# An attention kernel with a shorter way for the softmax shifts, a row norm in three parts, and its DFT spread over a block

## The chip, the cores and the metric

The kernel runs on one core of a Trainium2 chip. The metric is device time in microseconds (us), the median of three runs. PE is the TensorE engine, DVE is VectorE, ACT is ScalarE, POOL is GpSimd and SP is SyncE, whose queue issues most of the DMAs.

## What is computed

One layer (`DEPTH = 1`) over 4096 tokens of width 1024, with 16 meta tokens put ahead of them. Cut to what matters:

```python
u    = rmsnorm(h, norm_g)
proj = u @ w_in
f_in, f_gate, q, k, v, a_gate = split(proj)
f_out = fourier_branch(f_in, w_fmix, b_fmix) * silu(f_gate)
q, k  = rope(rmsnorm(q)), rope(rmsnorm(k))
a_out = softmax(q @ k.T / 8) @ v
h = h + concat(f_out, a_out * silu(a_gate)) @ w_out
return rmsnorm(h, final_g)[:, 16:]
```

There are 8 query heads and 2 key heads of width 64. The Fourier branch is a 2-D DFT over positions and channels, then a linear map per group.

## The kernel before

Every product of float32 numbers is made as three matmuls of 16-bit halves, a high part and the rest.

**Phase A** takes the tokens in tiles of 128, norms and projects them, and writes q, k, v and the gates to memory. **Phase B** does the rest. Its DFT is a list `flist` of 18 units of some 50 matmuls each ("pd" tiles), which `f_step(n, mid)` issues n at a time; each piece of its coefficients (`ct`) is a load of 1088 KB, and `mix` ends a unit with a product on POOL (`mo`, L834). Units are fed in as filler beside other work.

**Attention** goes in 8 blocks of 512 queries. A block has 4 pairs of heads, so there are 32 pairs, numbered from 0 here. A pair is 66 steps: two heads times 33 key tiles, the 33rd being the 16 meta keys. A step of `step` is `qk`, two matmuls on PE (L977 with the high halves `qA`, L978 with `qB`), an exp on ACT (L981), a subtraction `rr` (L983, 128x512) on DVE or POOL, and `pvm`, nine small matmuls on PE (L998 to L1005). `pvm` runs four steps (`LAG`) after its `qk`, so the products of key tile 5 stand in step 9. The last `pvm` of a head is followed by the copy `tt` on ACT and the chain `ob` of four products on POOL (L1013 to L1016). `on_dve` puts the `rr` of two steps after each place of the table `AT` on DVE, the others on POOL.

**The shifts.** Exp needs a maximum per query. While a pair runs, `max_units` finds those of the next pair: `grp` is two matmuls of 64 rows (L922) and a DVE reduce (L923), two groups at each step of `AT`; `meta` does the meta keys (L930, L932), `red` reduces to `mm` and scales to `nm` (L937, L938), and `fin` brings `nm` into rows 64 and up of `qB`: eight matmuls (L945) and two ACT copies (L948). Row 64 of `qB` meets a row of 256 in K, so L978 of a pair's first step adds the shift and needs the row to be there.

**The output projection** of a block runs in the four pairs of the next block, 128 tokens in each. At step `TR` `out_tr` transposes (L1041, into a bank of the same ring of two as the groups use) and splits (`mh` on ACT, `ml` on DVE, L1045); `out_units` puts one matmul (L1058) into each of 24 steps from `O0` and from `O1`; the sum with x is `hh` (L1063, DVE). At step 2 of the following pair `out_end` norms the tile: square on ACT (L1073), the root in ten small instructions on DVE (L1074 to L1092), then the scaled product `yo` on DVE (L1077) and its DMA.

**Block 0** has no output projection. Its 264 steps take in the rest of the DFT (`block0`, five matmuls a step from step 6 on), and after that the eight pieces of `w_out` are loaded (`wo_load`) and split on ACT and DVE (`wo_prep`, L909, L910).

**Between** phase A and block 0 lies a prelude: 50 DFT matmuls, the loads `qP` (query rows for the maxima), `wst`, `sgn` and `bias` for `fix_prep` (small DVE work on the DFT's first rows), the rest of K, then the 33 groups of pair 0 with DFT matmuls between them.

The order of work on an engine is the order of the code. The lines that set it here:

```python
AT = [0, 4, 8, 12, 15, 19, 22, 26, 29, 33, 36, 40, 43, 47, 50, 53, 56]
TR, O0, O1 = 8, 13, 41
last = {58: red, 61: fin}
on_dve = {j + 2 for j in AT}
```

Of the kernel before, what the change touches and what calls it, by code (L numbers as in the profile page):

```python
# [126 lines left out]
def phase_a(tc, a, pool, mm3, id16, id32, sc):  # L127
# [15 lines left out]
    with ExitStack() as st:  # L143
# [392 lines left out]
        early = sorted(order[:done])  # L536
        runs = [(t, t + 1) for t in early if t == NT]
        for t in early:
            if t < NT:
                if runs and runs[-1][1] == t and runs[-1][0] < NT:  # L540
                    runs[-1] = (runs[-1][0], t + 1)
                else:
                    runs.append((t, t + 1))
        at(done * 4 + 2 - 3 * 4, ld["k_load"], runs)
        ld["rest"] = sorted(order[done:])
# [118 lines left out]
def phase_b(tc, a, pool, mm3, id32, id16, sc):  # L664
# [10 lines left out]
    with ExitStack() as st:  # L675
# [14 lines left out]
        nm = [bp.tile([P, 2, 4, 32], F16, name=f"nm{i}") for i in range(2)]  # L690
# [41 lines left out]
        mo = w2.tile([P, 2, 512], F32, tag="ob", name="mo")  # L732
# [179 lines left out]

        def max_units(i):
            b, p = pairs[i]
            kv, q, n = p // 2, qP[b % 2], nm[i % 2]
            mx = sm.tile([P, 4, 2, 9], F32, tag="mx", name="mx")
# [8 lines left out]
            def meta():  # L925
                t = pm.tile([P, 2, 512], F32, tag="m", name="m")
                for e in range(2):
                    rs = slice(64 * e, 64 * e + 64)
                    for s in range(4):
                        T.matmul(t[:, e, s * 16:s * 16 + 16], q[rs, s, p], K[kv][rs, NT, 0, :NMETA],  # L930
                                 start=s == 0, stop=True, skip_group_check=s > 0)
                V.tensor_reduce(mx[:, :, :, 8], t[:, :, :64].rearrange("p e (s k)->p s e k", s=4),  # L932
                                axis=AX.X, op=ALU.max)

            def red():
                m = sm.tile([P, 4, 2], F32, tag="mm", name="mm")
# [15 lines left out]
            return [(lambda s=s, c=c: grp(s, c)) for s, c in order], meta, red, fin  # L952
# [171 lines left out]
        def block0(g, mid):  # L1124
# [5 lines left out]
            if g >= 6:  # L1130
                f_step(5, 1 if mid else 0)
# [252 lines left out]
```

## Time and profile before

| | before |
|---|---|
| median of three runs | 3383.28 us |
| the profiled execution: its own time, its span | 3382.96 us, 3381.2 us |
| phase A | 0 to 732 us |
| prelude | 732 to 824.5 us |
| pairs 0 to 3 (block 0) | 91.7, 97.8, 92.2 and 74.0 us |
| pairs 4 to 30 | 75.3 us, then 76.9 to 77.1 us each |
| pair 31 and the tail | 65.7 us and 58 us |
| busy over the span | PE 97%, DVE 70%, POOL 66%, ACT 51% |

The lengths of the pairs are distances between their first rows of L977. A row of the timeline gives the start, the duration, the engine, line, operation and tile, and in brackets the idle time of the engine ahead of it and what ended that. Matmuls overlap, so what one costs is the distance from its start to the next start.

### The profile page before, as it was taken

What the parts mean: (1) busy time and instruction counts of PE and PEld (TensorE: products, weight loads), DVE (VectorE), ACT (ScalarE), POOL (GpSimd) and SP (SyncE); (2) the same over time, 40 slices, a digit from 0 to 9 for tenths busy, and PEclk for the clock granted to TensorE, in tenths of its full rate; (3) what the DMA queues carried; (4) which work ended last, traced back from release to release, by engine and by line L of the source; (5) the groups of instructions that cost most, each with busy time, mean ns of one, the idle gap of its engine ahead of it and who ended that gap; (6) DMA issues with size and microseconds to landing.
All of it is one profiled execution on the core that took longest, in us unless ns stands there. A gap on an engine that the chain in (4) does not pass through costs nothing.

```text
span 3381.2 us, 79026 instructions
## 1 busy us (share of the span) xinstructions
PE 3278.4 (97%) x33332; PEld 1909.9 (56%) x33332; DVE 2368.1 (70%) x3249; ACT 1736.6 (51%) x3018; POOL 2226.8 (66%) x2131
## 2 busy tenths in 40 slices
PE   7999999988999999999999999999999999999998
PEld 3655555546676555555555555555555555555554
DVE  6666565537667877777777777777777776777764
ACT  5443443322555655555555555555555555555553
POOL 3655555323667877777777777777777777777762
PEclk9999999989999999999999999999999999999999
DMA  6444443437431110010001000200100010010001
GB/s 211 153 156 138 143 145 126 130 114 211 134 121 50 51 51 27 20 45 20 20 20 45 20 20 25 59 20 20 45 20 20 20 45 20 20 39 20 20 20 57
DMA packets 142298, 223.61 MB, mean 66 GB/s; under 512 B 30358, under 2 KB 85478, under 8 KB 137590
## 3 DMA queue, kind: packets, MB, share of 16 engines
q1 hardware_dynamic: 128118, 193.38, 18.3%
q10 hardware_dynamic: 13824, 25.17, 2.0%
q8 instruction: 261, 4.28, 0.5%
q14 instruction: 95, 0.78, 0.1%
HBM read 157.38 MB, written 61.14 MB: 65 GB/s over the span
## 4 chain that ended last, share of the span: by engine, by line
PE 67%; DVE 6%; issue 2%; ACT 1%; POOL 0%; ACTq 0%; POOLq 0%; DVEq 0%
PE s L977 12%; PE s L978 12%; PE o L998 11%; PE po L1058 9%; PE m L922 7%; PE o L1005 7%; PE pd L769 2%; PE o L1003 2%; PE o L1001 2%; DVE mx L923 1%; DVE yo L1077 1%; PE m L1217 1%; PE m L1041 1%; DVE r1t L1091 1%; DVE rf L1092 1%
## 5 line engine op out<-in xcount | busy, mean ns | idle before, releaser
L983 POOL TENSOR_TENSOR rr<-pe 128x512 f16<-128x512 f32 (+1 forms) x1541 | 1637.0, 1077 | 627.2 <-ACT pe L981 620.6
L981 ACT ACTIVATE pe<-s 128x512 f32<-128x512 f32 (+1 forms) x2112 | 1260.3, 597 | 1037.5 <-PE s L978 1011.1
L923 DVE TENSOR_REDUCE mx<-m 128x2 f32<-128x1024 f32 x1024 | 1206.1, 1217 | 260.8 <-PE m L922 256.9
L1005 PE MATMUL o<-VV,rr 128*128 128x65 f16 x8448 | 974.7, 193 | 1.1 <-POOL rr L983 0.5
L1005 PEld LDWEIGHTS <-rr 128*128 128x128 f16 x8448 | 784.4, 98 | 186.7 <-POOL rr L983 12.3
L998 PE MATMUL o<-VV,pe 128*128 128x129 f16 x6336 | 842.1, 222 | 14.1 <-ACT tt L1009 11.2
L998 PEld LDWEIGHTS <-pe 128*128 128x128 bf16 x6336 | 587.0, 97 | 390.5 <-issue 223.4
L977 PE MATMUL s<-qA,K 128*128 128x512 f16 (+1 forms) x2112 | 800.6, 379 | 0.3 <-ACT pe L981 0.2
L978 PE MATMUL s<-qB,K 128*128 128x512 f16 (+1 forms) x2112 | 800.3, 379 | 0.3 <-ACT qB L948 0.3
L983 DVE TENSOR_TENSOR rr<-pe 128x512 f16<-128x512 f32 x571 | 488.6, 857 | 222.0 <-ACT pe L981 219.0
L1001 PE MATMUL o<-VV,pe 128*128 128x65 f16 (+1 forms) x2112 | 411.0, 195 | 0.0
L1003 PE MATMUL o<-VV,pe 128*128 128x64 f16 (+1 forms) x2112 | 410.1, 194 | 0.0
L84 PE MATMUL ps<-wh,xh 128*128 128x512 f16 (+2 forms) x1032 | 365.7, 354 | 13.6 <-ACT xh L285 13.6
L86 PE MATMUL ps<-wh,xl 128*128 128x512 f16 (+2 forms) x1032 | 365.5, 354 | 2.5 <-POOL xl L286 2.5
L85 PE MATMUL ps<-wl,xh 128*128 128x512 f16 (+2 forms) x1032 | 365.5, 354 | 2.4 <-DVE wl L268 2.4
L922 PE MATMUL m<-K,qP 64*128 64x512 f16 x2048 | 321.1, 383 | 25.7 <-DMA bias<-bias 11.9
L922 PEld LDWEIGHTS <-qP 64*128 64x128 f16 x2048 | 66.2, 94 | 252.9 <-issue 244.7
L1003 PEld LDWEIGHTS <-pe 128*128 128x128 bf16 (+1 forms) x2112 | 208.7, 99 | 0.0
L977 PEld LDWEIGHTS <-K 128*128 128x128 f16 (+1 forms) x2112 | 202.8, 96 | 8.3 <-issue 1.4
L1001 PEld LDWEIGHTS <-pe 128*128 128x128 bf16 (+1 forms) x2112 | 206.2, 98 | 0.0
L978 PEld LDWEIGHTS <-K 128*128 128x128 f16 (+1 forms) x2112 | 204.6, 97 | 1.4 <-issue 1.3
L1058 PE MATMUL po<-wol,mh 128*128 128x512 f16 x448 | 170.1, 380 | 0.0
(191 smaller groups left out, 3575.6 us busy)
## 6 DMA issues: line engine op xcount, KB each, us to landing
ct<-cd SPq DMA_DIRECT2D x16, 1088.0 KB
room<-x SPq DMA_DIRECT2D x32, 512.0 KB
xt<-xt SPq DMA_DIRECT2D x32, 512.0 KB
sg<-fx SPq DMA_DIRECT2D x16, 1024.0 KB
xr<-x SPq DMA_DIRECT2D x32, 512.0 KB
out<-yo SPq DMA_DIRECT2D x32, 512.0 KB
fg_d<-g ACTq DMA_DIRECT2D x32, 256.0 KB
ag_d<-g ACTq DMA_DIRECT2D x32, 256.0 KB
```

Of the source, the lines that this page charges most:

```text
L84: T.matmul(out, lh, rh, start=first, stop=False, skip_group_check=skip)
L922: T.matmul(t[:, e], q[rs, s, p], K[kv][rs, 4 * c:4 * c + 4, 0], start=True, stop=True)
L923: V.tensor_reduce(mx[:, s, :, c], t, axis=AX.X, op=ALU.max)
L977: T.matmul(s[:n], K[kv][:, t, 0, :n], qa, start=True, stop=False)
L978: T.matmul(s[:n], K[kv][:, t, 1, :n], qb, start=False, stop=True)
L981: S.activation(pe[:n], s[:n], AF.Exp, scale=HD ** -0.5)
L983: eng.tensor_tensor(out=rr[:n], in0=pe[:n], in1=hi[:n], op=ALU.subtract)
L998: T.matmul(o[:, c0:c0 + 129], hi[:n, cs], va, start=t == 0 and s == 0, stop=t == NT, skip_group_check=True)
L1001: T.matmul(o[:, c0:c0 + 65], hi[:n, cs], vh, start=False, stop=t == NT, skip_group_check=True)
L1003: T.matmul(o[:, c0:c0 + 64], hi[:n, cs], vl, start=False, stop=t == NT, skip_group_check=True)
L1005: T.matmul(o[:, c0:c0 + 65], rr[:n, cs], vh, start=False, stop=t == NT, skip_group_check=True)
L1058: T.matmul(d["po"], (ml if w == 2 else mh)[:, i], wol[i // 4][:, i % 4, cs] if w == 1 else woh[0][:, i, cs], start=j == 0, stop=j == 23)
```

## The change

It has six parts. **Shifts:** `nm` is one 128x32 tile, `fin` is one matmul at step 63, and a new `put` at step 64 spreads its 8 rows over rows 64 to 71 of `qB` by a product with a unit matrix on DVE; K has 256 in eight rows. **Meta keys:** their maxima are taken once a block for all four pairs (`MT`, step 60 of the pair ahead; for block 0 two pairs at a time), and `red`, now at step 61, takes the minimum with them. **Norm in three parts:** at step 0 the square on ACT and the product `yo` of `hh` and the gain on POOL, at step 2 the root on DVE, at step 5 a scale of `yo` on ACT and the DMA. **Tables:** `AT` has 16 places with two groups each, `TR` is 11, `O0` 14. **Prelude:** the loads of the query rows and of `fix_prep` stand ahead of the first 50 DFT matmuls, `fix_prep` and the rest of K behind the first two groups. **Block 0:** three DFT matmuls a step in place of five, so that they last to step 231 and not 170 of the 264; the pieces of `w_out` are loaded two ahead and split every five steps, the last ones in pair 4.

On SP's queue, where phase A goes over into the prelude, before (`fgu` and `ct` belong to the DFT, `q_d` and `k_d` are q and k in memory):

```order
L822 DMA fgu<-fg_d 121x512
L822 DMA fgu<-fg_d 128x512
L105 DMA ct<-cd 128x4352
L701 DMA qP_7745<-q_d 64x4x512 x2
L738 DMA wst<-wst 128x1024
L739 DMA sgn<-sgn 128x2
L740 DMA bias<-bias 128x512
L118 DMA K_6582<-k_d 128x256 x6
L822 DMA fgu<-fg_d 128x512 x2
```

and now:

```order
L189 DMA k_d<-ko 128x512 x2
L704 DMA qP_7745<-q_d 64x4x512 x2
L741 DMA wst<-wst 128x1024
L742 DMA sgn<-sgn 128x2
L743 DMA bias<-bias 128x512
L825 DMA fgu<-fg_d 121x512
L825 DMA fgu<-fg_d 128x512
L105 DMA ct<-cd 128x4352
L825 DMA fgu<-fg_d 128x512 x2
L118 DMA K_6582<-k_d 128x2x256
L118 DMA K_6582<-k_d 128x4x256
```

The query rows and `bias` stand ahead of `fgu` and `ct`, and the rest of K is two loads and not six.

On DVE at the end of a steady pair and the start of the next, before:

```order
L932 TENSOR_REDUCE mx<-m 128x8
L983 TENSOR_TENSOR rr<-pe 128x512
L937 TENSOR_REDUCE mm<-mx 128x8
L938 TENSOR_SCALAR nm_7748<-mm 128x8
L1063 SCALAR_TENSOR_TENSOR hh<-po,xr 128x512
L923 TENSOR_REDUCE mx<-m 128x2 x2
L983 TENSOR_TENSOR rr<-pe 128x512
L1074 TENSOR_SCALAR ss<-ss 128x1
```

and now:

```order
L1003 TENSOR_TENSOR rr<-pe 128x512
L951 TENSOR_REDUCE mm<-mx 128x8
L952 SCALAR_TENSOR_TENSOR nm_7748<-mm,met 128x8
L1083 SCALAR_TENSOR_TENSOR hh<-po,xr 128x512
L964 TENSOR_TENSOR qB_7744<-m,id_70 8x2x4x128
L929 TENSOR_REDUCE mx<-m 128x2 x2
L1003 TENSOR_TENSOR rr<-pe 128x512
L1100 TENSOR_SCALAR ss<-ss 128x1
```

`put` (`qB`, 8x2x4x128) stands behind `hh` and ahead of the next pair's first groups; nothing of the meta keys is left there.

On POOL around the start of a pair (the 16x512 `rr` is the last key tile of the pair that ends), before:

```order
L983 TENSOR_TENSOR rr<-pe 128x512 x20
L983 TENSOR_TENSOR rr<-pe 16x512
L983 TENSOR_TENSOR rr<-pe 128x512 x3
L1013 TENSOR_TENSOR ob<-tt 128x3x64
L1014 TENSOR_TENSOR ob<-ob,ag 128x3x64
L1015 TENSOR_TENSOR ob<-tt,ag 128x64
L1016 TENSOR_TENSOR ob<-ob,rc 128x4x64
L983 TENSOR_TENSOR rr<-pe 128x512 x21
```

and now:

```order
L1003 TENSOR_TENSOR rr<-pe 128x512 x21
L1003 TENSOR_TENSOR rr<-pe 16x512
L1003 TENSOR_TENSOR rr<-pe 128x512
L1097 TENSOR_TENSOR yo<-hh,fgb 128x1024
L1003 TENSOR_TENSOR rr<-pe 128x512 x2
L1033 TENSOR_TENSOR ob<-tt 128x3x64
L1034 TENSOR_TENSOR ob<-ob,ag 128x3x64
L1035 TENSOR_TENSOR ob<-tt,ag 128x64
L1036 TENSOR_TENSOR ob<-ob,rc 128x4x64
L1003 TENSOR_TENSOR rr<-pe 128x512 x21
```

The norm's product of 128x1024 now stands behind the `rr` of step 0 and ahead of those of steps 1 and 3.

The diff, cut to its core:

```diff
-            G.memset(t[:, :, 1, 1, 0:1], 256.0)
+            G.memset(t[:, :, 1, 1, 0:8], 256.0)
-        nm = [bp.tile([P, 2, 4, 32], F16, name=f"nm{i}") for i in range(2)]
+        nm = [bp.tile([P, 32], F16, name=f"nm{i}") for i in range(2)]
+            mo = mos[:, 2 * (u // 2 % 2):2 * (u // 2 % 2) + 2]
             def meta():
+                ps = range(4) if b else range(p, p + 2)
...
+                mb = met[b][:, :, ps[0]:ps[-1] + 1]
+                V.tensor_reduce(mb, t[:, :, 64 * ps[0]:64 * ps[-1] + 64].rearrange("p e (x s k)->p e x s k", s=4, k=16),
                                 axis=AX.X, op=ALU.max)
+                V.tensor_scalar(out=mb, in0=mb, scalar1=-1.0 / 256.0, scalar2=None, op0=ALU.mult)
             def red():
                 m = sm.tile([P, 4, 2], F32, tag="mm", name="mm")
                 V.tensor_reduce(m, mx, axis=AX.X, op=ALU.max)
-                V.tensor_scalar(out=n[:, :, :, 0], in0=m.rearrange("p s e->p e s"), scalar1=-1.0 / 256.0,
-                                scalar2=None, op0=ALU.mult)
+                V.scalar_tensor_tensor(out=n[:, 0:8].rearrange("p (e s)->p e s", s=4),
+                                       in0=m.rearrange("p s e->p e s"), scalar=-1.0 / 256.0,
+                                       in1=met[b][:, :, p], op0=ALU.mult, op1=ALU.min)
             def fin():
                 t = pm.tile([P, 2, 512], F32, tag="m", name="m")
-                for e in range(2):
-                    for s in range(4):
-                        T.matmul(t[64:96, e, s * P:(s + 1) * P], n[:, e, s], id16, start=s == 0, stop=True,
-                                 skip_group_check=s > 0)
-                for e in range(2):
-                    S.activation(qB[b % 2][64:96, :, 4 * e + p], t[64:96, e].rearrange("p (s c)->p s c", s=4),
-                                 AF.Copy)
+                T.matmul(t[64:96, 0, :P], n, id16, start=True, stop=True)
+                rowt.append(t)
+            def put():
+                t = rowt.pop()
+                V.tensor_tensor(
+                    out=qB[b % 2].rearrange("p s (e q) c->p e s q c", e=2)[64:72, :, :, p],
+                    in0=t[64:72, 0, :P].unsqueeze(1).unsqueeze(1).broadcast_to([8, 2, 4, P]),
+                    in1=id32[64:72, 64:72].rearrange("p (e s)->p e s", s=4).unsqueeze(3).broadcast_to([8, 2, 4, P]),
+                    op=ALU.mult)
...
+            def square():
+                S.activation(xr, hh, AF.Square, accum_out=ss)
+                G.tensor_tensor(out=yo, in0=hh, in1=fgb[0], op=ALU.mult)
+            def root():
+                V.tensor_scalar(out=ss, in0=ss, scalar1=1.0 / D, scalar2=EPS, op0=ALU.mult, op1=ALU.add)
+                rsqrt1(sm, rf, ss)
+            def scale():
+                S.activation(yo, yo, AF.Copy, scale=rf)
+                t0 = b * QB + s * P
+                dma(a["out"][t0:t0 + P], yo)
+            return {0: square, 2: root, 5: scale}
...
-        AT = [0, 4, 8, 12, 15, 19, 22, 26, 29, 33, 36, 40, 43, 47, 50, 53, 56]
-        TR, O0, O1 = 8, 13, 41
+        AT = [0, 4, 8, 14, 18, 22, 26, 29, 33, 37, 41, 44, 48, 51, 55, 58]
+        MT, TR, O0, O1 = 60, 11, 14, 41
-        f_step(50, 0)
         qload(0, (0,))
         fix_load()
-        ld["k_load"]([(t, t + 1) for t in ld["rest"]])
-        fix_prep()
+        f_step(50, 0)
...
-            f_step(18, 1)
+            f_step(17, 1)
             n += 1
+            if n == 1:
+                fix_prep()
+                ld["k_load"](ld["rest"])
...
-            if g >= 6:
-                f_step(5, 1 if mid else 0)
+            if 6 <= g < 4 * 66:
+                f_step(3, 1 if mid else 0)
...
-                wo.extend((g + 2, (4 * 66 - 6 - g) // ND))
+                wo.extend((g + 2, 5))
+                wo_load(0)
+                wo_load(1)
                 d, r = divmod(g - wo[0], wo[1])
-                if 0 <= d < ND and r == 0:
-                    wo_load(d)
                 if 0 <= d < ND and r == wo[1] - 1:
                     wo_prep(d)
+                    if d + 2 < ND:
+                        wo_load(d + 2)
...
-                last = {58: red, 61: fin}
+                last = {61: red, 63: fin, 64: put}
```

## Rows read from the trace of the kernel before

**Rows 1.** Windows: us, busy PE, PEld, DVE, ACT, POOL (instructions), clock, DMA share, GB/s.

```profile
732.00:824.50 92.50, 68.15 (x607) 49.54 (x606) 55.36 (x59) 14.46 (x33) 25.29 (x16) 0.89 0.64 198
1064.00:1106.20 42.20, 39.21 (x491) 23.60 (x489) 30.98 (x33) 23.75 (x43) 34.01 (x31) 1.00 0.18 64
1106.20:1180.20 74.00, 67.04 (x812) 38.37 (x809) 67.47 (x61) 46.94 (x78) 62.43 (x58) 1.00 0.16 51
1332.40:1409.50 77.10, 75.77 (x868) 43.16 (x865) 57.99 (x68) 43.31 (x74) 56.77 (x58) 1.00 0.07 22
```

**Rows 2.** Waits: us in total, times, the longest.

```profile
PE m L922 <- DMA bias<-bias: 11.9, 1, 11.9
```

**Rows 3.** Timeline of SP's queue, start of the prelude.

```profile
738.72 1.28 SPq L701 DMA_DIRECT2D qP<-q_d  x2
```

**Rows 4.** Timeline of PE, head of pair 13.

```profile
1871.48 0.38 PE L977 MATMUL s<-qA,K 128*128 128x512 f16 x1
1871.69 0.38 PE L978 MATMUL s<-qB,K 128*128 128x512 f16 x1
...
1872.90 0.38 PE L977 MATMUL s<-qA,K 128*128 128x512 f16 x1
...
1875.46 0.39 PE L977 MATMUL s<-qA,K 128*128 128x512 f16 x1
...
1876.99 0.22 PE L998 MATMUL o<-VV,pe 128*128 128x129 f16 x1 [0.39 <-ACT tt L1009]
...
1879.69 0.38 PE L977 MATMUL s<-qA,K 128*128 128x512 f16 x1
...
1881.11 0.66 PE L1041 MATMUL m<-id,mf 128*128 128x128 f32 x4 [0.83 <-DVE mx L923]
...
1882.93 0.38 PE L977 MATMUL s<-qA,K 128*128 128x512 f16 x1
...
1883.71 0.38 PE L977 MATMUL s<-qA,K 128*128 128x512 f16 x1
```

**Rows 5.** Groups by line in pair 3: busy us, mean ns, idle time ahead.

```profile
L910 DVE SCALAR_TENSOR_TENSOR wol<-wot,woh 128x1024 f16<-128x1024 f32 x7 | 11.0, 1573 | 1.3 <-ACT woh L909 1.1
```

**Rows 6.** Timeline of PE, steps 61 and 62 of pair 12.

```profile
1865.83 0.38 PE L977 MATMUL s<-qA,K 128*128 128x512 f16 x1
...
1867.48 0.38 PE L977 MATMUL s<-qA,K 128*128 128x512 f16 x1
...
1868.48 0.38 PE L977 MATMUL s<-qA,K 128*128 128x512 f16 x1
```

**Rows 7.** Timeline of ACT, start of pair 13.

```profile
1872.17 0.60 ACT L981 ACTIVATE pe<-s 128x512 f32<-128x512 f32 x1 [0.36 <-PE s L978]
...
1874.87 1.05 ACT L1073 ACTIVATE xr<-hh 128x1024 f32<-128x1024 f32 x1
```

**Rows 8.** Timeline of DVE, end of pair 12 and start of pair 13.

```profile
1870.33 0.69 DVE L1063 SCALAR_TENSOR_TENSOR hh<-po,xr 128x512 f32<-128x512 f32 x1 [5.13 <-PE po L1058]
...
1876.04 0.15 DVE L1074 TENSOR_SCALAR ss<-ss 128x1 f32<-128x1 f32 x1 [0.19 <-ACT xr L1073]
...
1878.35 1.50 DVE L1077 SCALAR_TENSOR_TENSOR yo<-hh,rf,fgb 128x1024 f32<-128x1024 f32 x1
```

**Rows 9.** One line of DVE: count, duration ns least, median, most, span.

```profile
L1045 DVE TENSOR_TENSOR ml<-m,mh x28: 1209/1225/1225, 1190.5 to 3270.0; 128x1024 f16<-128x1024 f32 x28
```

**Rows 10.** Timeline of POOL: `ob` in mid-pair, then five `rr` in a row.

```profile
1839.37 0.53 POOL L1013 TENSOR_TENSOR ob<-tt 128x192 f32<-128x192 f32 x1
...
1841.52 4.49 POOL L983 TENSOR_TENSOR rr<-pe 128x512 f16<-128x512 f32 x4
...
1868.99 5.02 POOL L983 TENSOR_TENSOR rr<-pe 128x512 f16<-128x512 f32 x5 [0.76 <-ACT pe L981]
```

**Rows 11.** Timeline of POOL and of DVE, end of the prelude.

```profile
821.48 2.34 POOL L834 TENSOR_TENSOR mo<-mo,fgu 128x1024 f32<-128x1024 f32 x1 [3.32 <-DVE mm L937]
...
821.52 2.34 DVE L938 TENSOR_SCALAR nm<-mm 128x8 f16<-128x8 f32 x1
```

More of the change, by code (lines that the diff above doesn't have):

```diff
@@ L535, in phase_a, with runs @@
         done = 27
[L536 to L545, printed above, removed]
+        def runs(ts):
+            out = [(t, t + 1) for t in ts if t == NT]
+            for t in sorted(ts):
+                if t < NT:
+                    if out and out[-1][1] == t:
+                        out[-1] = (out[-1][0], t + 1)
+                    else:
+                        out.append((t, t + 1))
+            return out
+        at(done * 4 + 2 - 3 * 4, ld["k_load"], runs(order[:done]))
+        ld["rest"] = runs(order[done:])
         def deal(slot):
@@ L731, in phase_b @@
         thl = w1.tile([P, 2, 2, 4, P], F16, tag="yo", name="thl")
[L732 removed]
+        mos = w2.tile([P, 4, 512], F32, tag="ob", name="mo")
         fgs = {}
@@ L911, in wo_prep @@
                                    op0=ALU.mult, op1=ALU.subtract)
+        met, rowt = {}, []
         def max_units(i):
@@ L937, in red @@
                 V.tensor_reduce(m, mx, axis=AX.X, op=ALU.max)
-                V.tensor_scalar(out=n[:, :, :, 0], in0=m.rearrange("p s e->p e s"), scalar1=-1.0 / 256.0,
-                                scalar2=None, op0=ALU.mult)
+                V.scalar_tensor_tensor(out=n[:, 0:8].rearrange("p (e s)->p e s", s=4),
+                                       in0=m.rearrange("p s e->p e s"), scalar=-1.0 / 256.0,
+                                       in1=met[b][:, :, p], op0=ALU.mult, op1=ALU.min)
             def fin():
                 t = pm.tile([P, 2, 512], F32, tag="m", name="m")
-                for e in range(2):
-                    for s in range(4):
-                        T.matmul(t[64:96, e, s * P:(s + 1) * P], n[:, e, s], id16, start=s == 0, stop=True,
-                                 skip_group_check=s > 0)
-                for e in range(2):
-                    S.activation(qB[b % 2][64:96, :, 4 * e + p], t[64:96, e].rearrange("p (s c)->p s c", s=4),
-                                 AF.Copy)
+                T.matmul(t[64:96, 0, :P], n, id16, start=True, stop=True)
[7 more added lines that the diff above has]
+                    op=ALU.mult)
             order = [(s, c) for c in (0, 3, 4, 7, 1, 2, 5, 6) for s in range(4)]
-            return [(lambda s=s, c=c: grp(s, c)) for s, c in order], meta, red, fin
+            first = p == 0 or (b == 0 and p == 2)
+            return [(lambda s=s, c=c: grp(s, c)) for s, c in order], [meta] if first else [], red, fin, put
         obs = {}
@@ L1120, in phase_b @@
         fin()
+        put()
         wo = []
@@ L1147, in phase_b @@
                 qload(b + 1)
-            if b > 0:
+            if i > 4:
                 out_load(b - 1, p)
+            elif i == 4:
+                load_mf(0, 0)
             gs, last = [], {}
             if i + 1 < len(pairs):
-                gs, meta, red, fin = max_units(i + 1)
-                gs.append(meta)
-                last = {58: red, 61: fin}
+                gs, meta, red, fin, put = max_units(i + 1)
+                last = {61: red, 63: fin, 64: put}
+                if meta:
+                    last[MT] = meta[0]
             halves = None
@@ L1176, in phase_b @@
                     last[j]()
-                if i < 4:
+                if i < 5:
                     block0(66 * i + j, j - 2 in AT)
+                if i == 4 and j == 28:
+                    load_xr(0, 0)
                 if j == LAG + 2 and i + 1 < len(pairs):
@@ L1184, in phase_b @@
                     load_xr(b, 0)
-                if j == 2 and prev:
-                    out_end(*prev)
+                if j == 0:
+                    ends = out_end(*prev) if prev else {}
                     prev = None
+                if j in ends:
+                    ends[j]()
                 pend.append(pvm)
@@ L1246, in phase_b @@
         tail_mm(1, 0)
-        out_end(*prev)
+        for f in out_end(*prev).values():
+            f()
         load_xr(b, 1)
```

38 lines of the change are left out of this document (17 added, 21 removed).

## The prediction

> **What bounds the kernel now.** I read the windows first, then the waits, then single steps in the timelines. In a steady pair PE is busy for 75.77 of 77.10 us at the full clock [rows 1], so such a pair gets shorter only where PE waits or has less to do. Pair 3 is another thing: PE 67.04 and DVE 67.47 of 74.00 [rows 1], two engines that take turns in waiting. In the prelude PE works 68.15 of 92.50 us at a mean granted clock of 0.89 [rows 1], and half of its idle time is one wait of 11.9 us for `bias` [rows 2]. So the change can give something in three places: the prelude, block 0, and the 26 pairs from 5 to 30, where each microsecond counts 26 times.
>
> PE's prices, from the starts of steps [rows 4]: a bare step takes 0.78 us (1882.93 to 1883.71), one with two groups 1.42 (1871.48 to 1872.90).
>
> **Prelude.** `qP` is issued at 738.72 [rows 3], behind a `ct` of 1088 KB and the `fgu` pieces, and 50 DFT matmuls don't cover its landing. The change puts these loads ahead of `fgu` and `ct` and ahead of the 50 matmuls, so the 11.9 us go if the loads land within the matmuls. The late `fix_prep` and the rest of K then come behind the first groups; 17 DFT matmuls instead of 18 an iteration move work into block 0, where it still has to be done. I take −12. It is −8 if `fix_prep` or K delays the first iterations by 4 us, and −14 if some of the slow clock goes too: a mean of 0.89 over 92.5 us is about 20 us at 1.2 GHz and the rest at 2.4, and the pause of 11.9 us is the longest there is.
>
> **Block 0.** Pair 3 by its steps: 66 x 0.78 + 33 groups x 0.32 = 62, with the meta keys and `fin` some 64 us; it takes 74.00, so 10 us are waits. The end of pair 2, where the DFT is already out, loses 3 more (42.20 less 39.21) [rows 1]. DVE is why: besides groups and `rr` it makes the splits of `w_out`, at 1573 ns [rows 5]. With three matmuls a step, some 33 bare steps are left, with about 8 places of groups and six splits: on DVE 8 x 2.4 + 8 x 1.1 + 6 x 1.5 = 37 us, on PE 33 x 0.78 + 8 x 0.64 = 31. So about 4 to 6 us of 13 stay, and the four `fin` give 1.6 more (below). I take −11, with −6 if the waits only move, and −14 if all go. The fill is the same number of matmuls and costs nothing itself; two splits that slide into pair 4 lie on a DVE that is no bound there (57.99 of 77.10 [rows 1]).
>
> **The steady pair, what goes.** (1) `fin`: the step with eight matmuls takes 1.65, the next, the same without them, 1.00 [rows 6]; one matmul and the same change of array shape at both ends leave about 0.25, so −0.40. (2) The transposes at `TR` wait 0.83 for the reduce of an earlier group (0.99 by the starts) [rows 4], since DVE made the root and `yo`, 1876.04 to 1879.85 [rows 8]. `yo` leaves DVE and `TR` comes three steps later: −0.99, or −0.5 if DVE is still behind. (3) Step 4 takes 1.88 where 1.42 is usual, as `tt` is late [rows 4] behind the 1.05 us square on ACT [rows 7]. With the square at step 0 this goes, −0.45. (4) In mid-pair, at step 37, PE waits for the first head's `tt` in the same way, and a group now stands there to fill it; no row shows it apart, and I estimate half of the 0.45, some −0.25, between 0 and −0.45. Places, groups and meta keys come out even: 32 meta matmuls a block either way. In all −0.40 −0.99 −0.45 −0.25, or −2.1.
>
> **What comes.** (5) `put` stands behind `hh`, which ends at 1871.02 [rows 8], and L978 of the next pair's first step, which stood at 1871.69 [rows 4], needs it. No row has `put`. Its 1024 elements per partition are as many as those of `ml`, 1.225 us [rows 9]; `hh`, with 512, takes 0.69. I take 1.22, as the number of elements is the same: ready at 1872.24, a wait of 0.57. The bounds are 0.1 (priced as `hh`) and 1.1 (1.8 us, the two prices in a row).
>
> (6) POOL has to make `yo`, 128x1024. The same kind of product, `mo`, takes 2.34 [rows 11]; I take that. `rr` comes each 1.0 us (five in 5.02), `ob` takes 2.15 in mid-pair (1839.37 to 1841.52) [rows 10]. POOL can start `rr` of step 0 about 1.4 us after the pair's first matmul (its exp starts at 1872.17 and takes 0.6 [rows 7]), with the wait of (5) at 1.95. Up to `rr` of step 5 it has five `rr`, `ob`, `yo` and some 0.45 us in which DVE's own `rr` of step 2 holds it up: 5.0 + 2.15 + 2.35 + 0.45 = 9.95, so it is ready at 11.9. PE wants it in step 9. Step 9 stood 11.45 behind the pair's start (1871.48 to 1882.93); less the 0.45 of (3) and the 1.82 by which the transposes' step exceeded a step with groups, plus two matmuls and the wait of (5), that makes 10.2. PE waits 1.7. The scale on ACT, 1.0 us as the square, falls in the same time: its exps are late, but `rr` is later still, so it adds nothing. In all +2.27, so +0.17 a pair, 26 x 0.17 = +4. The reason to expect no gain here in spite of four waits removed is this queue on POOL.
>
> Pair 4, pair 31 and the tail I cost at nothing: pair 4 is bounded by the same steps, and pair 31 has no groups, so DVE is idle enough there.
>
> **Sum.** −12 −11 +4 = −19 against the profiled execution's 3382.96: 3364 us. The median of the runs is 0.3 us above that execution, which changes nothing.
>
> **A rule beside the row.** At the end of the prelude `nm` on DVE, 128x8, lasts 2.34 us and ends with the `mo` product on POOL that began 0.04 before it [rows 11]: the two engines shut each other out. By this row the 2.35 us of `yo` on POOL can hold a DVE instruction too. The Trainium skill, page "SBUF — State Buffer", section "Who interferes with whom", states that DVE and GpSimd share one pair of ports, that a DVE instruction with two SBUF inputs contends with GpSimd's reads, and that whoever issues first keeps it for the whole instruction. By that rule `put`, with one input in PSUM, does not wait for POOL, and DVE's `rr` of step 2 does: it speaks against moving `yo` to POOL.
>
> **Rivals.** A is the forecast. **B, POOL has room:** `put` is as short as `hh` (0.69) and `rr`'s queue is absorbed, as PE waits for something else by then. For it: POOL is busy only 56.77 of 77.10 us [rows 1]. Against it: the sum of (6), in which nothing but the queue counts. With 0.9 of new waits a pair gains 1.2, 26 x 1.2 = 31: 3383 − 23 − 31 = 3329. **C, slower by the lock on DVE:** `yo` on POOL starts at about 3 us into the pair and holds DVE's `rr` of step 2 until 5.3; behind that stand the root (2.3 us [rows 8]), `rc`, the next groups, and the scale on ACT that waits for the root; behind the scale all exps from step 6 on. If the scale runs from 8.3 to 9.3 in place of about 7, the exps of steps 6 to 8, and with them `rr` on POOL, are some 1.5 us later: new waits 3.75, +1.65 a pair, 26 x 1.65 = 43, so 3383 − 23 + 43 = 3403. It decides from +1.15 a pair on: 26 x 1.15 = 30 undoes the 23 and the 0.2%. The Trainium skill, page "Perfetto Trace Analysis", section "Optimizing Scalar/DVE Operations", says of the same shared port that moving work between GpSimd and DVE might not help; by that rule C, or A without the gain of (2), is what happens; in rows of this case only the 2.34 us of `nm` bear it out, one instance. **D, the early gains don't come:** `q_d` is written by phase A's last tiles, so `qP` may wait for it at the queue's head and hold `ct` and `fgu` back, and the waits of pair 3 spread over pairs 1 to 3. With a third of the 23 us left and +4 in the pairs: 3379.
>
> **Chances.** A 0.50, B 0.25, C 0.12, D 0.13. A's own range is 3350 to 3378 (3 us for the prelude, 4 for block 0, 0.4 a pair). The range 3326 to 3390 holds A, D and two thirds of B, and leaves out the rest of B and most of C, 0.18 together. About 0.2%, 6.8 us, is what a measurement of this kernel can tell from no change: Faster by more: A in nine of ten cases, B in all, D in one of six, 0.45 + 0.25 + 0.02 = 0.72. Slower by more: C in five of six, D in one of six, A in one of fifty, 0.10 + 0.02 + 0.01 = 0.13. The rest, 0.15, is the same.
>
> **What would show it.** The wait of 11.9 for `bias` is gone and the first groups start by about 740; pair 3 is near 66 and no pair of block 0 is longer than 98; the transposes' wait for `mx` and that for `tt` vanish from the head, and in their place L978 of step 0 waits some 0.6 for `put`, and the products of steps 8 to 10 some 1.7 for POOL's `rr`; `put` lasts 1.2, `yo` on POOL 2.35. Steady pairs of 77.2 show A, 75.8 B, 78.6 C. I am wrong if `put` or POOL's `yo` has another price by half, or if the pairs change by over 0.5 us either way.

## The result, and the profile after

The changed kernel takes 3388.85 us, median of 14 runs, against 3383.27 for the kernel before: a ratio of 1.0018, interval [1.0011, 1.0025]. It is 5.6 us slower, 0.18%. That is inside the range that was given, but the forecast was faster. The profiled execution took 3392.44 us, span 3390.7, so 3.6 us over the median. Some of this lies in the prelude, where TensorE ran at 1.2 GHz for 10.2 us (0 to 6.8 in the other profiles with this prelude), and some in pair 3, 96.1 us long, where the profiles of runs 3, 4 and 7 below have 94.1 to 94.6 with the same code.

The page of the changed kernel, its span and its busy times:

```profile
span 3390.7 us, 78607 instructions
PE 3273.2 (97%) x33108; PEld 1893.9 (56%) x33108; DVE 2349.4 (69%) x3208; ACT 1727.1 (51%) x2982; POOL 2294.0 (68%) x2190
```

The engines' shares say nothing; the stages do. Distances between the pairs' first qk matmuls, in us:

| | start of pair 0 | pairs 0 to 3 | pair 4 | pairs 5 to 30, mean | pair 31, to the first matmul of the tail's projection |
|---|---|---|---|---|---|
| before | 824.5 | 91.7, 97.8, 92.2, 74.0 | 75.3 | 77.01 | 68.4 |
| changed | 814.7 | 84.1, 89.9, 87.3, 96.1 | 77.6 | 77.41 | 73.1 |
| difference | −9.8 | +1.7 together | +2.3 | +0.40, or +10.3 | +4.7 |

Pair 31 is counted here to 3326.18 before and 3335.40 now; the 65.7 us above end a little behind its last qk. The differences make +9.2 of the 9.5 us between the spans. The windows that answer to [rows 1], and the last pair, in the changed kernel:

```profile
732.00:814.70 82.70, 67.34 (x610) 49.85 (x608) 55.59 (x60) 15.74 (x34) 24.88 (x16) 0.94 0.68 221
1076.00:1172.10 96.10, 87.34 (x1002) 50.42 (x999) 67.41 (x69) 48.03 (x85) 68.97 (x65) 0.95 0.17 54
1326.80:1404.20 77.40, 75.37 (x853) 42.53 (x851) 57.20 (x67) 43.13 (x73) 59.17 (x60) 1.00 0.07 22
3262.30:3332.00 69.70, 65.76 (x778) 42.46 (x776) 38.05 (x57) 42.68 (x72) 32.22 (x33) 0.98 0.07 24
```

In the prelude PE's idle time fell from 24.4 to 15.4 us. In the steady pair PE has 0.4 us less work than before and waits 0.7 us more. Pair 3 and pair 31 now run below the full clock, which they did not before.

Block 0 as a whole and pair 4, before and now:

```profile
824.50:1180.20 355.70, 345.01 (x4053) 219.41 (x4053) 253.14 (x258) 193.28 (x348) 257.24 (x244) 1.00 0.31 96
1180.20:1255.50 75.30, 75.20 (x867) 42.80 (x864) 55.24 (x57) 42.43 (x72) 56.72 (x59) 1.00 0.16 43
```

```profile
814.70:1172.10 357.40, 346.55 (x4043) 217.34 (x4043) 246.92 (x255) 183.50 (x333) 257.26 (x249) 0.98 0.29 91
1172.10:1249.70 77.60, 75.15 (x853) 42.33 (x850) 62.02 (x60) 44.65 (x74) 59.51 (x58) 1.00 0.23 66
```

PE is idle for 10.7 us of block 0 before and for 10.9 now, and in pair 4 for 0.1 before and 2.4 now. The change did not take the waits out of this stretch.

**The head of a steady pair.** In the changed kernel L997 and L998 are the qk, L1001 the exp, L1003 `rr`, L928 and L929 the groups, and L1025 a product with `rr`. The timeline of PE, where it waits, and of DVE, POOL and ACT at the same time (pair 6):

```profile
1327.70 0.38 PE L998 MATMUL s<-qB,K 128*128 128x512 f16 x1 [0.47 <-DVE qB L964]
...
1336.69 0.38 PE L997 MATMUL s<-qA,K 128*128 128x512 f16 x1 [0.94 <-ACT pe L1001]
...
1339.24 0.20 PE L1025 MATMUL o<-VV,rr 128*128 128x65 f16 x1 [0.47 <-POOL rr L1003]
```

```profile
1326.42 1.22 DVE L964 TENSOR_TENSOR qB<-m,id 8x1024 f16<-8x1024 f32 x1
...
1331.01 1.73 DVE L1003 TENSOR_TENSOR rr<-pe 128x512 f16<-128x512 f32 x1 [0.21 <-ACT pe L1001]
...
1334.84 0.17 DVE L1031 RECIPROCAL rc<-tt 128x4 f32<-128x4 f32 x1
```

```profile
1329.84 2.35 POOL L1097 TENSOR_TENSOR yo<-hh,fgb 128x1024 f32<-128x1024 f32 x1
1332.15 2.49 POOL L1003 TENSOR_TENSOR rr<-pe 128x512 f16<-128x512 f32 x2
```

```profile
1335.00 1.15 ACT L1104 ACTIVATE yo<-yo,rf 128x1024 f32<-128x1024 f32 x1 [0.81 <-DVE rc L1031]
1336.06 1.06 ACT L1001 ACTIVATE pe<-s 128x512 f32<-128x512 f32 x2
```

The old waits, for the transposes and for `tt` [rows 4], are gone. Three are new. `put` makes L998 wait, 0.64 by the starts. POOL's product from 1329.84 to 1332.19 holds DVE's `rr` of step 2, which takes 1.73 and not 0.69; the root ends 1 us later, the scale starts at 1335.00 and two exps come behind it: PE waits 1.1 by the starts, at the qk of step 8. POOL's `rr` of steps 1 and 5 are late as well, 0.95 in the two places together.

**The end of block 0.** SP, ACT and PE in pair 3:

```profile
1120.61 17.39 SPq L841 DMA_DIRECT2D mf_d<-mo  x6
1138.05 0.36 SPq L1166 DMA_DIRECT2D fgb<-fgb  x1
1138.45 36.36 SPq L909 DMA_DIRECT2D wot<-wo  x7
```

```profile
1143.82 1.06 ACT L913 ACTIVATE woh<-wot 128x1024 f16<-128x1024 f32 x1 [4.43 <-DMA wot<-wo]
```

```profile
1145.41 0.59 PE L997 MATMUL s<-qA,K 128*128 128x512 f16 x1 [3.92 <-ACT pe L1001]
...
1146.35 1.04 PE L928 MATMUL m<-K,qP 64*128 64x512 f16 x4
...
1168.25 0.23 PE L959 MATMUL m<-id,nm 128*32 128x128 f16 x1 [2.37 <-DVE nm L952]
```

The first piece of `w_out` is asked for at 1138.45, behind the DFT's last stores `mf_d` in SP's queue and behind `fgb`; the DFT's last matmul starts at 1124.57. ACT stops for the piece, its exps stand behind, and PE stands still for 3.9 us. After that L997 takes 0.59 where 0.38 is usual: the granted clock is at 1.2 GHz, and the mean of pair 3 is 0.95. At the pair's end `fin` waits 2.4 for DVE, and the clock falls again.

### The profile page after: what moved, and what is told of

The parts are those of the page before. It is cut to its first block, busy times and chain, and to the rows that moved or that the text cites. A ratio compares the mean times of both kernels' runs of the same rounds, so it can differ in the third digit from the quotient of the medians.

```text
span 3390.7 us, 78607 instructions
## 1 busy us (share of the span) xinstructions
PE 3273.2 (97%) x33108; PEld 1893.9 (56%) x33108; DVE 2349.4 (69%) x3208; ACT 1727.1 (51%) x2982; POOL 2294.0 (68%) x2190
## 4 chain that ended last, share of the span: by engine, by line
PE 63%; POOL 9%; DVE 2%; issue 1%; ACT 1%; DMA 1%; SPq 0%; POOLq 0%; ACTq 0%; DVEq 0%
PE s L997 12%; PE s L998 11%; PE o L1018 11%; PE po L1078 9%; PE o L1025 7%; PE m L928 6%; POOL rr L1003 5%; PE pd L772 2%; POOL yo L1097 2%; PE o L1023 2%; PE o L1021 2%; PE m L1256 1%; PE m L1061 1%; ACT pe L1001 1%; POOL ob L1034 0%
## 5 line engine op out<-in xcount | busy, mean ns | idle before, releaser
L1003 POOL TENSOR_TENSOR rr<-pe 128x512 f16<-128x512 f32 x1572 | 1671.9, 1078 | 587.4 <-ACT pe L1001 580.0
L1001 ACT ACTIVATE pe<-s 128x512 f32<-128x512 f32 (+1 forms) x2112 | 1256.0, 596 | 1093.6 <-PE s L998 1050.3
L929 DVE TENSOR_REDUCE mx<-m 128x2 f32<-128x1024 f32 x1024 | 1204.5, 1218 | 317.8 <-PE m L928 316.7
L1025 PE MATMUL o<-VV,rr 128*128 128x65 f16 x8448 | 977.5, 193 | 17.8 <-POOL rr L1003 14.0
L1025 PEld LDWEIGHTS <-rr 128*128 128x128 f16 x8448 | 783.3, 98 | 188.7 <-POOL rr L1003 36.2
L1018 PE MATMUL o<-VV,pe 128*128 128x129 f16 x6336 | 851.1, 222 | 0.2 <-ACT tt L1029 0.2
L997 PE MATMUL s<-qA,K 128*128 128x512 f16 (+1 forms) x2112 | 802.8, 380 | 31.4 <-ACT pe L1001 31.4
L998 PE MATMUL s<-qB,K 128*128 128x512 f16 (+1 forms) x2112 | 802.9, 380 | 13.8 <-DVE qB L964 13.8
L1003 DVE TENSOR_TENSOR rr<-pe 128x512 f16<-128x512 f32 x540 | 463.5, 859 | 204.6 <-ACT pe L1001 203.6
L928 PE MATMUL m<-K,qP 64*128 64x512 f16 x2048 | 314.0, 383 | 9.3 <-DVE mo L836 4.5
L998 PEld LDWEIGHTS <-K 128*128 128x128 f16 (+1 forms) x2112 | 204.9, 97 | 35.1 <-issue 35.1
L997 PEld LDWEIGHTS <-K 128*128 128x128 f16 (+1 forms) x2112 | 203.0, 96 | 8.0 <-issue 1.2
L928 PEld LDWEIGHTS <-qP 64*128 64x128 f16 x2048 | 62.1, 94 | 246.3 <-issue 239.3
L286 POOL TENSOR_TENSOR xl<-xt,xh 128x1024 f16<-128x1024 f32 (+1 forms) x33 | 68.7, 2082 | 153.8 <-ACT xh L285 148.0
```

What stands on the lines that cost most here:

```text
L928: T.matmul(t[:, e], q[rs, s, p], K[kv][rs, 4 * c:4 * c + 4, 0], start=True, stop=True)
L929: V.tensor_reduce(mx[:, s, :, c], t, axis=AX.X, op=ALU.max)
L997: T.matmul(s[:n], K[kv][:, t, 0, :n], qa, start=True, stop=False)
L998: T.matmul(s[:n], K[kv][:, t, 1, :n], qb, start=False, stop=True)
L1001: S.activation(pe[:n], s[:n], AF.Exp, scale=HD ** -0.5)
L1003: eng.tensor_tensor(out=rr[:n], in0=pe[:n], in1=hi[:n], op=ALU.subtract)
```

## The experiments

Each edit is made in the changed kernel unless another is named; times are medians, the kernel before took 3381.8 to 3383.7 beside them.

**1. The first pieces of w_out early.**

```diff
+            if g == 200:
+                wo_load(0)
+                wo_load(1)
             if 6 <= g < 4 * 66:
                 f_step(3, 1 if mid else 0)
...
-                wo_load(0)
-                wo_load(1)
```

> The changed kernel, but the first two pieces of w_out are loaded at step 200 of block 0 and not behind the DFT's last stores at step 231. Theory L (the load is late): the changed kernel's ACT waited 4.4 us for the first piece, PE then 3.9 us for exps queued behind it, and the granted clock was 0.5 for 6.8 us after that, 3.4 us of loss. With the load early, pair 3 goes from 96.1 to about 88 us and the time falls by 7 (5 to 10). Rival (DVE bounds the end of block 0 anyway, as before): the wait moves to the groups and splits that stand behind each other on DVE, and less than 3 us is gained.

3385.83 us, ratio to before 1.0007 [0.9997, 1.0017], 3 us under the changed kernel. The wait for the piece is gone, and the clock falls once in pair 3, not twice. Pair 3 takes 92.0, where the four profiles with the late load and the same code (the changed kernel's, runs 3, 4 and 7) have 94.1 to 96.1. So the late load cost some 3 us, less than half of what Theory L took, and at the edge of what the rival allowed. Pair 3 is still 18 us longer than before; half of its steps now hold DFT matmuls, and the three pairs ahead of it are shorter for that. What is left to gain stands on DVE at the pair's end:

```profile
1157.49 0.68 DVE L945 TENSOR_REDUCE met<-m 128x32 f32<-128x512 f32 x1
1158.20 1.01 DVE L947 TENSOR_SCALAR met<-met 128x32 f32<-128x32 f32 x1
1159.13 1.21 DVE L914 SCALAR_TENSOR_TENSOR wol<-wot,woh 128x1024 f16<-128x1024 f32 x1
1160.26 0.20 DVE L951 TENSOR_REDUCE mm<-mx 128x8 f32<-128x64 f32 x1
1160.50 0.76 DVE L952 SCALAR_TENSOR_TENSOR nm<-mm,met 128x8 f16<-128x8 f32 x1
1161.58 1.22 DVE L964 TENSOR_TENSOR qB<-m,id 8x1024 f16<-8x1024 f32 x1 [0.32 <-PE m L959]
```

The meta keys of the next block, a split and the reduction follow each other ahead of `fin`, and DVE has no gap in them.

**2. fin and put one step earlier.**

```diff
-                last = {61: red, 63: fin, 64: put}
+                last = {61: red, 62: fin, 63: put}
```

> The changed kernel with fin at step 62 and put at step 63, so that put stands ahead of the sum hh on DVE. Theory P (put behind hh is late): the second qk matmul of a pair's first step waited 0.64 by the starts; that goes, and since exps and POOL's queue of the head start with that step, all of it is gained: 27 pairs x 0.6 = 16 us less (11 to 18). Rival (the wait is hidden by POOL's queue, which is late anyway): the products' wait for rr grows by as much, and the time changes by less than 4.

3477.86 us, 1.0282 [1.0266, 1.0297]: neither. L998 of step 0 no longer waits, and the steady pairs rose to some 81 us. DVE, POOL and PE at the head of pair 8, and a window behind it:

```profile
1494.07 4.30 DVE L1003 TENSOR_TENSOR rr<-pe 128x512 f16<-128x512 f32 x1 [0.22 <-ACT pe L1001]
```

```profile
1492.98 2.35 POOL L1097 TENSOR_TENSOR yo<-hh,fgb 128x1024 f32<-128x1024 f32 x1
1495.30 2.03 POOL L1003 TENSOR_TENSOR rr<-pe 128x512 f16<-128x512 f32 x2
1497.30 0.52 POOL L1033 TENSOR_TENSOR ob<-tt 128x192 f32<-128x192 f32 x1
```

```profile
1502.31 0.59 PE L997 MATMUL s<-qA,K 128*128 128x512 f16 x1 [2.63 <-ACT pe L1001]
```

```profile
1501.40:1508.20 6.80, 5.89 (x38) 2.94 (x38) 4.91 (x6) 3.13 (x6) 5.45 (x5) 0.50 0.84 218
```

DVE's `rr` of step 2 was under way at 1494.07, with POOL's product running. Less the 0.69 that it usually takes, it came in only at about 1497.7: POOL went from the product to two `rr` and to `ob` without letting it in. Root, scale and exps are 3.4 us later, PE stands still for 2.6, and then runs at 1.2 GHz (0.50 in the window's clock) for 6.8 us. This is the chain of rival C, and more than C had: there `rr` was held to the end of the product, here 2.4 us beyond it. In the changed kernel the same `rr` got in after 1 us.

One steady pair of this run is a test of that. In pair 16 the `rr` got in behind the product:

```profile
2142.66 1.80 DVE L1003 TENSOR_TENSOR rr<-pe 128x512 f16<-128x512 f32 x1 [0.23 <-ACT pe L1001]
```

The clock does not fall there, and the pair takes 76.6 us, less than in the changed kernel; the other 25 steady pairs take 79.7 to 82.1.

**3. The scale on ACT later.**

```diff
-            return {0: square, 2: root, 5: scale}
+            return {0: square, 2: root, 10: scale}
```

> The changed kernel with the norm's scale on ACT at step 10 and not 5; the product on POOL stays at step 0. In the changed kernel step 7's qk waits 1.1 us for exps that are queued behind the scale, which waits for the root on DVE. Theory Q (POOL's queue bounds the head): that wait goes, but PE then waits for rr of steps 4 and 5 until about the same moment: 0 to 0.4 us a pair, 0 to 10 us in all, and 3 us more in pair 31. Rival (the scale on ACT bounds): 1.1 x 26 = 29 us less.

3392.13 us, 1.0025 [1.0016, 1.0034]. The steady pairs take 77.66 in the mean, where the changed kernel has 77.41. The rival's 29 us are out. Theory Q was nearer, but it had 0 to 10 us less, and the run is 3 us slower. In pair 6 the 1.1 at the qk of step 8 (the expectation says 7) is gone, and by the starts 1.1 for a group's bank, which DVE frees late, stands in its place, beside 0.96 for `rr` and 0.23 at step 13. Moving the last of the three steps alone buys nothing there; pair 31 got 2.7 us back.

**4. Product and scale away from the head.**

```diff
-                G.tensor_tensor(out=yo, in0=hh, in1=fgb[0], op=ALU.mult)
+            def prod():
+                G.tensor_tensor(out=yo, in0=hh, in1=fgb[0], op=ALU.mult)
...
-            return {0: square, 2: root, 5: scale}
+            return {0: square, 2: root, 16: prod, 24: scale}
```

> The changed kernel with the norm's product on POOL at step 16 and the scale on ACT at step 24, away from the head of the pair, where tt and the ob chain stand. Theory Q (the product is harmless, its place is what costs): the waits of the head for exps (1.1) and rr (0.95) go, 2.0 x 26 = 52 us less, and 3 us in pair 31; about 3334 us. Rival (POOL has no room for 2.35 us more, or the lock between POOL and DVE costs the same anywhere): a wait for rr of 1 us or more turns up around steps 18 to 24, and the gain is 25 us or less.

3341.96 us, 0.9877 [0.9862, 0.9892]. The same product, 47 us less, where Theory Q had 55 and the rival at most 25. The steady pairs fell by 1.56 (75.85 in the mean) and pair 31 by 4.7.

```profile
1339.17 2.87 POOL L1099 TENSOR_TENSOR yo<-hh,fgb 128x1024 f32<-128x1024 f32 x1
1341.99 6.49 POOL L1003 TENSOR_TENSOR rr<-pe 128x512 f16<-128x512 f32 x6
```

```profile
1329.64 0.39 PE L928 MATMUL m<-K,qP 64*128 64x512 f16 x2 [0.33 <-DVE mx L929]
```

The first two rows are POOL's, the third PE's. The product takes 2.87 here, with a DVE `rr` beside it, and PE waits for no `rr` behind it. The waits for exps and `rr` at the head are gone; one of 0.50 by the starts, for a bank at step 8, is new. As run 3 gained nothing by the scale alone, it is the place of the product that counts.

**5. The three edits together.** 1, 2 and 4 in one kernel.

> The changed kernel with the three edits together: w_out's first pieces early, fin and put one step earlier, the norm's product on POOL at step 16 and its scale on ACT at 24. Theory S (in the run with put early, DVE's rr of step 2 was shut out for 4.3 us by POOL's product and the POOL work queued right behind it, and everything else followed from that): without the product at the head put early now gains its 0.64 in 27 pairs, 17 us, and the early load 4: from 3342 to about 3321 (3315 to 3328). Rival (POOL's rr and ob at the head shut DVE out as well): the clock falls in every pair again, and the time is 3360 or more.

3327.63 us, 0.9836 [0.9821, 0.9851]: Theory S, at the upper end of its range. `put` early now gives 0.6 a pair (75.22 in the mean) without any fall of the clock in a steady pair. What it did in run 2 needed the product at the head.

**6. Run 2 with rr of step 2 on POOL.**

```diff
-            on_dve = {j + 2 for j in AT}
+            on_dve = {j + 2 for j in AT if j}
```

> The kernel with put early that took 3478 us, with rr of step 2 on POOL and not on DVE, so that DVE has no instruction there with two inputs in SBUF. Theory S: DVE's wait of 4.3 us and the clock's falls go, and with them some 90 us; POOL's queue is one rr longer, 11.9 us from the pair's start for rr of step 5 where PE wants it at 9.6, so 2.3 us of waits a pair in place of 2.7 in the changed kernel: 3378 us (3368 to 3395). Rival (POOL's queue itself stopped PE, and not the lock): it stays above 3440, as the queue is longer.

3421.04 us, 1.0115 [1.01, 1.013], between the two. DVE has no long `rr` at the head any more and the scale comes 5.9 us after the pair's first exp, not 9.4: 57 of the 89 us that run 2 lost went with that. The rest is POOL's queue and the clock. PE's waits for `rr` at the head come to 2.8 by the starts in pair 8, not far from the 2.3 expected; the longest:

```profile
1500.94 0.20 PE L1025 MATMUL o<-VV,rr 128*128 128x65 f16 x1 [1.90 <-POOL rr L1003]
```

What Theory S missed is the clock. In pair 8 it does not fall, and the pair takes 77.3 us, no more than in the changed kernel. In 20 of the 26 steady pairs it falls once, for 3.4 us, and these take 78.7 to 79.5.

**7. The product on DVE again.**

```diff
-                G.tensor_tensor(out=yo, in0=hh, in1=fgb[0], op=ALU.mult)
...
-                S.activation(yo, yo, AF.Copy, scale=rf)
+                V.scalar_tensor_tensor(out=yo, in0=hh, scalar=rf, in1=fgb[0], op0=ALU.mult, op1=ALU.mult)
...
-            return {0: square, 2: root, 5: scale}
+            return {0: square, 2: root}
```

> The changed kernel with the norm's product on DVE again, scaled in the same instruction at step 2; the square stays at step 0 on ACT. Theory Q (the norm's new place at the head is what costs): the waits for exps (1.1) and rr (0.95) go, and DVE, with TR three steps later, is late only for the groups of steps 4 and 8, by 0.3 to 0.8: 1.3 to 1.7 us a pair less, 3345 to 3355. Rival (DVE is as full as POOL, and the transposes wait for it again): 0.5 us a pair less at most, 3376 or more.

3378.48 us, 0.9984 [0.9974, 0.9993]. The rival's numbers held: 0.23 us a pair, and the rest of the 10 us in pair 31. The waits for exps and `rr` went, and PE waits 1.9 by the starts for the groups of step 8 instead (the transposes, which the rival named, do not wait): root and product end at 1330.89 on DVE, and the reduces of step 4's groups come after:

```profile
1332.15 0.39 PE L928 MATMUL m<-K,qP 64*128 64x512 f16 x2 [0.84 <-DVE mx L929]
1333.29 0.39 PE L928 MATMUL m<-K,qP 64*128 64x512 f16 x2 [0.74 <-DVE mx L929]
```

At the head, the product costs about the same on either engine: 77.18 a pair on DVE, 77.41 on POOL, and 75.85 with POOL's product later (run 4). So the place mattered more than the engine. Whether DVE's form would do as well at a later step was not tried.

**8. The old fill of block 0.** `f_step(5, ...)` and the old spacing of `w_out`.

> The changed kernel with the DFT at five matmuls a step in block 0 and w_out loaded and split at the old spacing. Theory L (as it stands, the new fill gives back in pair 3 what it gains, by the late load, the meta keys and splits ahead of fin, and the slow clock after both): block 0 takes its old 355.7 us, plus 3.7 for the 17 DFT matmuls moved out of the prelude, less 1.6 for fin, 358 where the change has 357.4: no difference, 0 to 3 us slower, and pair 4 is 2 us shorter. Rival (the new fill is worth the forecast 11 us, and block 0 is long for another reason): 8 us or more slower.

3382.62 us, 1.0 [0.9991, 1.0009], 6 us under the changed kernel. Neither theory had it faster. Pairs 0 to 4 took 92.2, 100.1, 88.9, 73.7 and 74.8, together 429.7; the new fill takes 433.3 to 435.0 in the changed kernel and runs 3, 4 and 7. The new fill is worth less than nothing as it stands.

**9. The splits away from the end of pair 3**, in the kernel of run 5.

```diff
-                wo.extend((g + 2, 5))
+                wo.extend((238, 243, 248, 266, 271, 276, 281, 286))
```

> The kernel with all three edits (3328 us), with w_out's splits at steps 238, 243 and 248 of block 0 and the other five in pair 4, steps 2 to 22, so that none stands among the last groups, the meta keys and red of pair 3. Theory L: with the early load alone, fin and the meta keys of pair 3 still waited 2.5 and 1.8 us for DVE, and the clock fell for 3.4 us behind that; these go, pair 3 is shorter by 4 to 6 us, pair 4 longer by 0 to 2: about 3323 us (3320 to 3326). Rival (the splits cost DVE the same anywhere): pair 4 takes on what pair 3 loses, 3327 or more.

3325.31 us, 0.9831 [0.9815, 0.9847]: pair 3 92.9 to 90.7, pair 4 77.7 to 78.6. Half of the expected gain, inside Theory L's range; but at 2.3 us the difference to run 5 is within the spread of the runs, so it does not decide between the two.

**10. The root later**, in the kernel of run 9.

```diff
-            return {0: square, 2: root, 16: prod, 24: scale}
+            return {0: square, 15: root, 16: prod, 24: scale}
```

> As the run before it, with the norm's root on DVE at step 15 and not 2. In the run with the product at step 16 one wait was left at the head, 0.50 us of a group for a bank that DVE frees late. Theory Q (it is late by the root, 2.3 us): that wait goes, 0.5 x 26 = 13 us less. Rival (DVE is behind at step 8 in any case, or falls behind at 14 to 18 instead): less than 4 us.

3320.17 us, 0.9815 [0.9801, 0.983]. 5 us less than run 9. The wait of 0.50 at step 8 went, and one of 0.29 for `rr` came at step 9; 0.2 us a pair. Neither theory's size: the next wait was close behind.

**11. The old prelude.** The 50 DFT matmuls first, `fix_prep` and K ahead of the groups, 18 an iteration.

> The changed kernel with the prelude's order of before (50 DFT matmuls first, then the query rows and the loads of fix_prep, fix_prep and the rest of K ahead of the groups, 18 DFT matmuls an iteration). Theory E (the early loads are worth what the traces show): the wait of some 12 us comes back, the first pair starts at about 824 in place of 808 to 815, block 0 is 3.5 shorter by the 17 matmuls: 6 to 12 us slower than the changed kernel, about 3397 us. Rival (given back later, as block 0 is held by loads): within 3 us of the changed kernel.

3400.06 us, 1.0051 [1.0036, 1.0066], 11 us slower than the changed kernel, as Theory E had it. The first pair starts at 824.5 and PE has the long wait again, of 12.13 us:

```profile
749.85 0.58 PE L928 MATMUL m<-K,qP 64*128 64x512 f16 x1 [12.13 <-DMA K<-k_d]
```

**12. The old fill in the kernel of run 10**, with loads early and splits twelve steps apart.

```diff
-                f_step(3, 1 if mid else 0)
+                f_step(5, 1 if mid else 0)
...
-                wo.extend((238, 243, 248, 266, 271, 276, 281, 286))
+                wo.extend((188, 200, 212, 224, 236, 248, 266, 276))
```

> The fastest kernel so far (root late, 3320 us) with the DFT at five matmuls a step again, the first two pieces of w_out loaded at step 150, and the eight splits at steps 188 to 248 of block 0, twelve apart, and at steps 2 and 12 of pair 4. Theory D (DVE has room for a split only beside many bare steps or in pair 4): pairs 0 to 4, which took 433.6 us there and 429.7 with the old fill and spacing, take 426 to 430: 4 to 7 us less, 3313 to 3316. Rival (three matmuls a step is the better fill once splits and loads are out of the way): 3320 or more.

3319.29 us, 0.9811 [0.9798, 0.9825]: pairs 0 to 4 take 432.4 where run 10 has 433.7. The rival said 3320 or more, and Theory D's 4 to 7 us did not come. Once loads and splits stand well, three or five matmuls a step make no difference that shows. It beats the kernel before by 1.9%.

## Why the prediction was wrong

By the traces, the −19 us of the sum came out as +9.2. Of the 28 us between them, block 0 and pair 4 are 15, the steady pairs 6, pair 31 5 and the prelude 2.

**Prelude, −12: right.** It was −9.8 in the profiled execution, and run 11 gives −11 in the medians, with the 17 DFT matmuls that went over to block 0 set against it. The start of pair 0 lies between 808.4 and 814.7 in the profiles with the new prelude.

**Block 0, −11: the step that failed.** It came to +1.7 (in the profiles of runs 3, 4 and 7, with the same code, to between −0.1 and +0.4), and pair 4, costed at nothing, to +2.3. The term took it that with the DFT spread out, 7 to 9 of 13 us of waits would go. They stayed: PE's idle time in block 0 is 10.7 us before and 10.9 now (9.4 to 9.6 in runs 3, 4 and 7), most of it in pair 3 in both. DVE is busy over pairs 0 to 4 for 308.4 us before and 308.9 now, which is the nearest reason; no run takes work off DVE there, so that is not shown. Four things are in the miss.

- The 17 DFT matmuls that moved out of the prelude were named and not entered in the sum. By the trace of run 11, where 16 of them take 1.86 us, they are 2 us, and not the 3.7 and 3.5 that two expectations above put.
- I priced the splits' work on DVE and not their loads. The queue on which they stand (SP's, behind the last `mf_d`) was not followed, some 3 us by run 1.
- The chain of meta keys, split and `red` ahead of `fin` met the backlog on DVE that I had counted. Behind this wait and that for the load PE ran at 1.2 GHz for 10.2 us of pair 3, where it did not before.
- Four splits and not two slid into pair 4, onto "a DVE that is no bound there". It is one: DVE is busy there for 62.0 us in place of 55.2, and PE is idle for 2.4 and not 0.1. Run 8, with all splits in block 0, has pair 4 at 74.8.

Beyond that the gain itself was not there: runs 8, 9, 10 and 12 put pairs 0 to 4 at 429.7 to 433.7 us in their arrangements, before 431.0. Splits that get out of pair 3 come back in part in pair 4 (run 9). The working was loose, too. Its 4 to 6 of 13 us that stay and the 1.6 of `fin` make 8.6 to 10.6, not 11; ten of the 13 came from prices of steps, where the windows of [rows 1] have 7.0 of idle time in pair 3. And the sign "pair 3 is near 66" overlooked that a DFT that lasts to step 231 fills half of pair 3.

**Steady pairs, +0.17: right in kind, short in size, +0.40.** What came is 2.7 by the starts (2.27 forecast); what went is then 2.3 (2.1). `put` lasts 1.22 us and costs 0.64, where 1.22 and 0.57 stood (its own starts give 0.55). POOL's product lasts 2.35, as taken. The wrong step is in (6): "The scale on ACT, 1.0 us as the square, falls in the same time: its exps are late, but `rr` is later still, so it adds nothing." PE waits 1.1 behind the scale, and as it comes late to POOL's `rr`, the wait there is 0.95 in place of 1.7. By run 3 the scale is not the whole of it: without it DVE frees the groups' bank as late. (6) counted 0.45 us in which DVE's `rr` holds up POOL, and nothing for POOL holding up DVE, 1 us in the changed kernel, behind which stand the root, the groups and the scale. This lock was given to rival C; run 2 shows it with 3.6. C had a chance of 0.12 and a price of 3403; its mechanism was part of the likeliest case.

**Pair 31, at nothing: +4.7.** There the root waits on DVE behind two `rr`, which take 3.86 us together beside POOL's product and `rr`; the scale at step 5 waits for the root, and all exps behind it. ACT's row and then PE's:

```profile
3271.94 1.15 ACT L1104 ACTIVATE yo<-yo,rf 128x1024 f32<-128x1024 f32 x1 [2.68 <-DVE rc L1031]
```

```profile
3273.62 0.38 PE L997 MATMUL s<-qA,K 128*128 128x512 f16 x1 [2.62 <-ACT pe L1001]
```

Behind this wait PE runs at 1.2 GHz for 3.4 us. With the scale at step 10 the pair gets back 2.7 (run 3), with the product late as well it is 68.4, as before (run 4).

**The rule beside the row.** The Trainium skill, page "SBUF — State Buffer", section "Who interferes with whom", states that a DVE instruction with at most one SBUF input, outside the 2-port modes, does not contend with GpSimd, and that one with two contends with a GpSimd instruction that reads SBUF. The trace agrees: `put`, with one input in PSUM, took 1.22 us in each of 32 cases, in 31 of them with POOL at work beside it, and DVE's `rr` beside the product took 1.73 in place of 0.69. Run 2 has more than the prediction drew from it, as the waiting DVE was passed over at three changes of POOL's instruction.

## What to carry to other kernels

Work that leaves a busy engine should be put where the receiving engine has slack in that stretch: the same product on POOL, with its scale, cost 47 us more at the head of the pair than 16 steps later. A step that is split into parts on three engines is a chain, and whatever stands in order behind its last part waits for the slowest; price that part with the wait in front of it. And when work is moved towards the end of a stage, follow its loads through their queue too.

## What was not expected of the hardware

An instruction on DVE with two inputs in SBUF can be held for longer than the POOL instruction it meets: 4.30 us where 0.69 is usual, past one product of 2.35, two `rr` and the start of `ob`. In the changed kernel it met the same instructions in the same order, and was held for 1.0. It starts 1.17 us behind the product there and 1.08 in run 2; but pair 16 of run 2, with 1.09, got in early too. What decides between the two stays open; it was not tried apart from the pair's head.

The clock counted for as much as the waits. Pauses of PE of 2.6 and 3.9 us were each followed by a stretch at 1.2 GHz, the 1.90 of run 6 in 20 steady pairs of 26, and the 1.1 of the changed kernel's steady pairs in none. In run 2 the stretches at 1.2 GHz within pairs 5 to 30 add up to 133 us. Half of that is lost where PE had work throughout: up to 66 of the 89 us.
